# Hybrid decoder trunk: tile 0 of each inner norm turned by VectorE's 32x32 blocks and a trip through DRAM

## The chip, the cores and the metric

The kernel runs on one core of a Trainium2 chip. A core has five engines with a queue each: TensorE (PE; its weight loads are listed as PEld), VectorE (DVE), ScalarE (ACT), GpSimd (POOL) and SyncE (SP), and 16 DMA engines that they share. Each engine works through its instructions in program order and waits on semaphores for the others. The metric is the device time of one execution in microseconds.

## What is computed

A decoder of two layers on x of 512 tokens by 1024 features, all in float32. Each of its four sub-layers stands between two RMS norms:

```
for layer in range(2):
    h = rms_norm(x, norm_mix_pre[layer])
    h = attention(h) if layer == 0 else rglru(h)
    x = x + rms_norm(h, norm_mix_post[layer])
    h = rms_norm(x, norm_ffn_pre[layer])
    h = conv_ffn(h)                       # up 1024 -> 6144, conv, gelu(g) * v, down 3072 -> 1024
    x = x + rms_norm(h, norm_ffn_post[layer])
```

rms_norm divides a token's 1024 features by the root of their mean square and multiplies by a gain per feature. The mixer of layer 0 is a dilated sliding-window attention (24 heads in three groups), that of layer 1 a gated linear recurrence.

## The kernel before

**Layout.** x stays in SBUF as x_sb: four token tiles (t = 0 to 3) of 128 tokens on the partitions, 1024 features along the row. The products of a sub-layer's first step need the features on the partitions, so what a norm gives is kept turned, as hT: eight blocks of 128 features by 512 tokens. Each float32 operand is split into a rounded part and a remainder (hi, lo; hT is such a pair), and each product is three matmuls (mm3, line 253): hi by hi, lo by hi, hi by lo.

**Weights.** They come in chunks of up to 1 MB on SP's queue (load, line 193) into three raw buffers, and are split into hi (ScalarE, line 149) and lo (VectorE, line 150) units by pump (line 167), with at most eight units live.

**Order of the work.** The program is written in the order in which each engine runs it. TensorE's work is cut into steps. After each step tick (line 222) is called: it lets the side jobs that are due go on, and then pump splits more weights if there is room for units. A side job is a generator; the number that it yields is the count of ticks until it goes on.

**The end of a sub-layer.** rows_run (line 422) computes the last product of a sub-layer, token tile by token tile, in PSUM banks called acc. An order written by hand says which tiles take which weight chunks: tiles 0 and 1 finish first, then 2, then 3. When a tile is complete, its norms (line 362) become a side job: postnorm (line 347) adds the normed result to x_sb, and prenorm (line 285) makes the next sub-layer's input. Three of the four sub-layers have a next one: these are the three *inner norms*, after attention, after the first FFN and after the recurrence.

**prenorm and transposed.** rms (line 257) takes the sums of squares on ScalarE and the root's correction on VectorE; the halves of the row, 512 features each, are multiplied by the gain (line 290) and by the root (line 294), into xs[0] and xs[1]. Then the job yields, 4 ticks for tiles 0 to 2 and 3 for tile 3, and transposed (line 298) follows: per half, four TensorE transposes of 128x128 into one PSUM bank (line 302, the tile tr), ScalarE's copy into hT's hi (line 306), and VectorE's subtraction into its lo (line 307).

A step of this stage has 12 matmuls. With the tick at which tile 0's norms are issued called 0, tile 0's transposes are issued at tick 4, tile 1's norms at 3 and its transposes at 7, tile 2's norms at 7, tile 3's at 9. From tick 7 until tile 3's norms are done, no weights are split ("hold", line 363). The next sub-layer's first step (feat_tiles with halves, line 380) follows tick 9: four products on tiles 0 and 1, 24 matmuls of 256 columns each, and then the same four on tiles 2 and 3. Tile 2's transposes stand between the second and the third product of the first round, tile 3's between the third and the fourth.

The gains are loaded on POOL's queue (line 136; on SP's at the end of attention) at the begin of rows_run. POOL also carries small loads of attention: a skewed bias matrix per head (toe, line 586) and, through a DRAM row, a factor per token (crow and cn, lines 813 and 815). The attention's values take a trip through DRAM on SP's queue, to be regrouped (vrows and vp, lines 685 and 698).

SBUF tiles of 128x512 float32 come from one pool of 28 buffers (gen, line 118); PSUM has eight banks.

Of the kernel before, what the change touches and what calls it, by code (L numbers as in the profile page):

```python
# [11 lines left out]
F32 = mybir.dt.float32  # L12
F32R = mybir.dt.float32r
I32 = mybir.dt.int32
AF = mybir.ActivationFunctionType
ALU = mybir.AluOpType
AX = mybir.AxisListType

P = 128
# [55 lines left out]
def kernel(  # L75
# [25 lines left out]
    nc = tc.nc  # L101
# [8 lines left out]
    dp = ctx.enter_context(tc.tile_pool(name="dp", bufs=1, space=bass.MemoryType.DRAM))  # L110
# [3 lines left out]
    def nm(s):  # L114
        uid[0] += 1
        return f"{s}{uid[0]}"

    def gen(dt=F32, s="g"):
        return gp.tile([P, 512], dt, tag="g", name=nm(s))

    def psum(s="ps"):
        return pp.tile([P, 512], F32, tag="ps", name=nm(s))
# [134 lines left out]
    def rms(parts, then):  # L257

        ss, b, v, y, q = small(2), small(2), small(1), small(1), small(1)
        for i, h in enumerate(parts):  # L260
            junk = gen(s="junk")
            nc.scalar.activation(junk, h, AF.Square, accum_out=ss[:, i : i + 1])  # L262
            then(i)
            if not i:
                nc.vector.tensor_scalar(b[:, 0:1], ss[:, 0:1], 1.0 / D, EPS, op0=ALU.mult, op1=ALU.add)
                nc.vector.tensor_scalar(b[:, 1:2], b[:, 0:1], -0.5, None, op0=ALU.mult)
        nc.scalar.activation(y, ss[:, 1:2], AF.Sqrt, scale=1.0 / D, bias=b[:, 0:1])
        nc.vector.scalar_tensor_tensor(v, ss[:, 1:2], -0.5 / D, b[:, 1:2], op0=ALU.mult, op1=ALU.add)
        nc.vector.reciprocal(y, y)
        nc.vector.scalar_tensor_tensor(q, y, v, y, op0=ALU.mult, op1=ALU.mult)  # L270
        nc.vector.scalar_tensor_tensor(y, q, 1.5, y, op0=ALU.add, op1=ALU.mult)
        return y
# [6 lines left out]
    def halves(ap):  # L279
        return [ap[:, 0:512], ap[:, 512:1024]]  # L280

    def new_hT():
        return tuple(htp.tile([P, KD, S], F32R, tag=f"hT{i}", name=nm(f"hT{i}")) for i in range(2))

    def prenorm(t, hT, g, wait):
        xh, gh = halves(x_sb[:, t, :]), halves(g)
        xs = [gen(s="xs") for _ in range(2)]

        def gained(i):
            nc.vector.tensor_tensor(xs[i], xh[i], gh[i], op=ALU.mult)  # L290

        y = rms(xh, gained)
        for i in range(2):
            nc.vector.tensor_scalar(xs[i], xs[i], y, None, op0=ALU.mult)
        yield wait
        transposed(t, xs, hT)

    def transposed(t, xs, hT):
        for i in range(2):
            ps = psum("tr")  # L300
            for k in range(4):
                nc.tensor.transpose(ps[:, k * P : (k + 1) * P], xs[i][:, k * P : (k + 1) * P], ident)  # L302
            ps3 = ps.rearrange("p (k c) -> p k c", k=4)
            hi = hT[0][:, 4 * i : 4 * i + 4, t * P : (t + 1) * P]
            lo = hT[1][:, 4 * i : 4 * i + 4, t * P : (t + 1) * P]
            nc.scalar.activation(hi, ps3, AF.Copy)
            nc.vector.tensor_tensor(lo, ps3, hi.bitcast(F32), op=ALU.subtract)
# [54 lines left out]
    def norms(t, banks, post_g, pre_g, hT):  # L362
        state["hold"] = t >= 2
        postnorm(t, banks, post_g, hT is None)
        if hT is not None:
            yield from prenorm(t, hT, pre_g, 3 if t == 3 else 4)
        if t == 3:
            state["hold"] = False
# [160 lines left out]
    def ffn(layer, hT, post, pre):  # L529
        ca, cc = ffn_cols[layer]  # L530

        def conv(ps, j):
            u = gen(s="u")
            nc.scalar.activation(  # L534
                u, ps, AF.Identity, scale=cc[:, j : j + 1], bias=cc[:, 48 + j : 49 + j]
            )
            for d, wc in ((1, ca[:, 48 + j : 49 + j]), (2, ca[:, j : j + 1])):
                nc.vector.scalar_tensor_tensor(  # L538
                    u[:, d:], ps[:, : S - d], wc, u[:, d:], op0=ALU.mult, op1=ALU.add
                )  # L540
            return u

        gv = []

        def sink(b, ps, j):
            m = b % 2
            if b < 2:
                u = conv(ps, 2 * j + m)
                nc.scalar.activation(u, u, AF.Gelu_apprx_tanh)  # L549
                gv.append(u)  # L550
            else:
                u = conv(ps, 24 + 2 * j + m)
                nc.vector.tensor_tensor(gv[2 * j + m], gv[2 * j + m], u, op=ALU.mult)

        order = [([0, 1, 2, 3], range(9)), ([0], range(9, 12)), ([1], range(9, 12))]
        order += [([2, 3], [9]), ([2], [10, 11]), ([3], [10, 11])]
        prep, run = rows_proj(12, act_split(gv), order, post, pre)
        for j in range(12):
            if j == 11:
                prep(3)  # L560
            feat_tiles(2, hT, lambda b, ps: sink(b, ps, j), j == 0)
        return run()
# [472 lines left out]
    hT = attention(hT, (norm_mix_post, 0), (norm_ffn_pre, 0))  # L1035
    hT = ffn(0, hT, (norm_ffn_post, 0), (norm_mix_pre, 1))
    hT = lru(hT, (norm_mix_post, 1), (norm_ffn_pre, 1))
# [29 lines left out]
```

## Time and profile before

| | us |
|---|---|
| median of three runs | 1474.26 (1474.23 to 1474.28) |
| the profiled execution | 1474.08 |
| its span, first to last instruction | 1472.3 |

| engine | busy share of the span |
|---|---|
| PE | 99% |
| PEld | 84% |
| DVE | 58% |
| ACT | 46% |

The mean TensorE clock granted was 0.999 of full speed. A line of a timeline has the start in us from the span's start, the duration in us, the engine, the line of the kernel, the operation, what it writes and reads, how many of them stand together, and in brackets how long the engine idled before and for whom. A line of a group has count, total busy us and mean ns. A line of a DMA issue has the count, the size of one and the median us from issue to landing. A line of the chain of work that ended last has start, us, engine, tile and line.

### The profile page before, as it was taken

What the parts mean: (1) busy time and instruction counts of PE and PEld (TensorE: products, weight loads), DVE (VectorE), ACT (ScalarE), POOL (GpSimd) and SP (SyncE); (2) the same over time, 40 slices, a digit from 0 to 9 for tenths busy, and PEclk for the clock granted to TensorE, in tenths of its full rate; (3) what the DMA queues carried; (4) which work ended last, traced back from release to release, by engine and by line L of the source; (5) the groups of instructions that cost most, each with busy time, mean ns of one, the idle gap of its engine ahead of it and who ended that gap; (6) DMA issues with size and microseconds to landing.
All of it is one profiled execution on the core that took longest, in us unless ns stands there. A gap on an engine that the chain in (4) does not pass through costs nothing.

```text
span 1472.3 us, 18613 instructions
## 1 busy us (share of the span) xinstructions
PE 1463.5 (99%) x7030; PEld 1231.3 (84%) x7030; DVE 847.1 (58%) x1888; ACT 679.6 (46%) x1538; POOL 43.2 (3%) x111
## 2 busy tenths in 40 slices
PE   9999999999999999999999999999999999999998
PEld 7888888888888898888888888988898888888886
DVE  5645546454545786555555337868785555565333
ACT  7645536262615454433444234489454333444321
POOL 0400001010100000000000000000000000000000
PEclk9999999999999999999999999999999999999999
DMA  6622235343434333223223231341323323223201
GB/s 203 198 65 89 91 91 140 112 137 113 127 125 130 118 115 114 87 91 110 86 106 124 86 99 44 122 138 58 110 97 108 101 86 114 87 87 129 100 0 58
DMA packets 116082, 154.39 MB, mean 105 GB/s; under 512 B 5208, under 2 KB 97592, under 8 KB 115992
## 3 DMA queue, kind: packets, MB, share of 16 engines
q1 hardware_dynamic: 112104, 144.72, 29.9%
q0 software_dynamic: 3296, 7.43, 2.5%
q8 instruction: 55, 0.90, 0.3%
q10 hardware_dynamic: 592, 1.05, 0.2%
q14 instruction: 35, 0.29, 0.1%
HBM read 146.81 MB, written 6.38 MB: 104 GB/s over the span
## 4 chain that ended last, share of the span: by engine, by line
PE 93%; ACT 4%; DVE 3%; issue 1%; DVEq 0%; ACTq 0%
PE ps L255 54%; PE acc L255 24%; PE v L673 7%; PE v L614 1%; DVE xb L879 1%; PE O L821 1%; PE S L774 1%; PE O L759 1%; PE S L724 1%; DVE wlo L150 1%; PE tr L302 1%; ACT sig L900 1%; ACT whi L149 1%; PE PT L808 0%; PE PT L746 0%
## 5 line engine op out<-in xcount | busy, mean ns | idle before, releaser
L255 PE MATMUL ps<-hT,whi 128*128 128x512 f32 (+1 forms) x2752 | 801.6, 375 | 0.0
L255 PEld LDWEIGHTS ps<-hT,whi 128*128 128x128 f32 x2752 | 503.2, 188 | 91.0
L255 PE MATMUL ps<-hT,wlo 128*128 128x512 f32 (+1 forms) x1376 | 515.2, 374 | 0.0
L150 DVE TENSOR_TENSOR wlo<-raw,whi 128x512 fp32r<-128x512 f32 x360 | 230.8, 686 | 190.1 <-ACT whi L149 190.1
L255 PEld LDWEIGHTS ps<-hT,wlo 128*128 128x128 f32 x1376 | 259.1, 188 | 46.5
L149 ACT ACTIVATE whi<-raw 128x512 fp32r<-128x512 f32 x360 | 204.7, 622 | 135.3 <-PE acc L255 120.9
L538 DVE SCALAR_TENSOR_TENSOR u<-ps,cols,u 128x511 f32<-128x511 f32 x192 | 143.8, 749 | 139.9 <-ACT u L534 136.5
L255 PE MATMUL acc<-whi,ahi 128*128 128x512 f32 x512 | 199.9, 390 | 0.0
L255 PE MATMUL acc<-whi,alo 128*128 128x512 f32 x512 | 199.4, 389 | 0.1
L255 PE MATMUL acc<-wlo,ahi 128*128 128x512 f32 x512 | 199.2, 389 | 0.0
L143 ACT ACTIVATE whi<-raw,first_w 128x128 fp32r<-128x128 f32 (+1 forms) x432 | 146.5, 427 | 62.4 <-PE ps L255 53.2
L534 ACT ACTIVATE u<-ps,cols 128x512 f32<-128x512 f32 x96 | 74.8, 779 | 209.3 <-PE ps L255 209.3
L144 DVE SCALAR_TENSOR_TENSOR wlo<-raw,first_w,whi 128x128 fp32r<-128x128 f32 (+1 forms) x432 | 141.9, 391 | 37.5 <-ACT whi L143 37.5
L255 PEld LDWEIGHTS acc<-whi,alo 128*128 128x128 f32 x512 | 96.1, 188 | 20.3 <-DVE alo L150 0.6
L255 PEld LDWEIGHTS acc<-wlo,ahi 128*128 128x128 f32 x512 | 96.2, 188 | 19.9
L255 PEld LDWEIGHTS acc<-whi,ahi 128*128 128x128 f32 x512 | 96.2, 188 | 19.7
L673 PE MATMUL v<-whi,hT 128*128 128x512 f32 x320 | 103.6, 395 | 0.0
L673 PEld LDWEIGHTS v<-whi,hT 128*128 128x128 f32 x320 | 60.1, 188 | 12.1
L549 ACT ACTIVATE u<-u 128x512 f32<-128x512 f32 x48 | 30.3, 632 | 81.2 <-DVE u L538 81.2
L673 PE MATMUL v<-wlo,hT 128*128 128x512 f32 x160 | 62.3, 390 | 0.0
L353 DVE TENSOR_TENSOR post<-acc,gain 128x512 f32<-128x512 f32 x32 | 22.0, 686 | 46.5 <-ACT junk L262 46.5
L601 DVE TENSOR_TENSOR qk<-ps,roots 128x512 f32<-128x512 f32 x24 | 16.6, 690 | 53.4 <-PE ps L255 53.4
(163 smaller groups left out, 969.2 us busy)
## 6 DMA issues: line engine op xcount, KB each, us to landing
raw<-in_ffn_w_up_dram SPq DMA_DIRECT2D x48, 1024.0 KB, 5.2
raw<-in_attn_w_qkv_dram SPq DMA_DIRECT2D x26, 1024.0 KB, 5.0
raw<-in_ffn_w_down_dram SPq DMA_DIRECT2D x24, 1024.0 KB, 5.0
raw<-in_attn_w_qkv_dram SPq DMA_DIRECT2D x19, 512.0 KB, 6.7
raw<-in_lru_w_in_dram SPq DMA_DIRECT2D x8, 1024.0 KB, 5.4
vrows<-v SPq DMA_DIRECT2D x16, 256.0 KB, 3.8
vp<-vrows SPq DMA_DIRECT2D x16, 256.0 KB, 3.7
raw<-in_attn_w_o_dram SPq DMA_DIRECT2D x4, 1024.0 KB, 5.0
```

What stands on the lines that cost most here:

```text
L143: nc.scalar.activation(hi[:, k], raw[:, k], AF.Copy, scale=w)
L144: nc.vector.scalar_tensor_tensor(lo[:, k], raw[:, k], w, hi[:, k].bitcast(F32), op0=ALU.mult, op1=ALU.subtract)
L149: nc.scalar.activation(hi, raw, AF.Copy)
L150: nc.vector.tensor_tensor(lo, raw, hi.bitcast(F32), op=ALU.subtract)
L255: mm(dst, l[a], r[b], start=start and n == 0, stop=stop and n == 2)
L302: nc.tensor.transpose(ps[:, k * P : (k + 1) * P], xs[i][:, k * P : (k + 1) * P], ident)
L353: nc.vector.tensor_tensor(u[i], parts[i], g[:, at[i]], op=ALU.mult)
L534: nc.scalar.activation(u, ps, AF.Identity, scale=cc[:, j : j + 1], bias=cc[:, 48 + j : 49 + j])
L538: nc.vector.scalar_tensor_tensor(u[:, d:], ps[:, : S - d], wc, u[:, d:], op0=ALU.mult, op1=ALU.add)
L549: nc.scalar.activation(u, u, AF.Gelu_apprx_tanh)
L601: nc.vector.tensor_tensor(dst, src, row, op=ALU.mult)
L673: mm(banks[t], hT[a][:, k, t * P : (t + 1) * P], W[b][:, k % 2, :], start=(k, a, b) == (0, 0, 0), stop=(k, a, b) == (KD - 1, 1, 0),)
```

## The change

For tile 0 of an inner norm TensorE's transposes go. Per half of 512 features:

1. `turned`: VectorE transposes each 32x32 block of xs in place of the whole, 128x512 in one instruction, into a tile T whose columns are ordered by (feature block of 32 within 128, block of 128, token within 32). T is written to a new DRAM tensor of 128x512 by one DMA on POOL's queue (256 KB).
2. `fetched`: four DMAs on POOL's queue read it back (64 KB each), each for 32 partitions: 128 rows of 512 bytes. In the tile that they fill, the features are on the partitions, and the columns are ordered by (token block of 32, block of 128 features, token).
3. ScalarE's copy to hi and VectorE's subtraction to lo read this tile in runs of 32 elements, from SBUF.

Steps 1 and 2 are issued right after the scaling (line 294), both writes ahead of the eight reads; step 3 comes six ticks later, where transposed came after four. Per inner norm that is two VectorE transposes and ten DMAs for eight TensorE transposes and two PSUM banks; the copies and subtractions keep their number. Tiles 1 to 3 stay as they were, and so does the first norm at the start of the kernel, which has functions of its own.

```diff
@@ -282,6 +282,26 @@
+    def turned(src, i):
+
+        T = gen(s="T")
+        nc.vector.transpose(
+            T.rearrange("p (c n j) -> p c n j", c=4, j=32), src.rearrange("p (n c j) -> p c n j", c=4, j=32)
+        )
+        d = dp.tile([P, 512], F32, name=nm("turned"))
+        nc.gpsimd.dma_start(d, T)
+        return d
+
+    def fetched(d):
+
+        t = gen(s="ft")
+        for c in range(4):
+            nc.gpsimd.dma_start(
+                t[32 * c : 32 * c + 32].rearrange("j (b x) -> j b x", b=4),
+                d.rearrange("(b j) (c x) -> c j b x", j=32, c=4)[c],
+            )
+        return t.rearrange("p (b n i) -> p n b i", b=4, i=32)
+
     def prenorm(t, hT, g, wait):
@@ -292,8 +312,17 @@
         y = rms(xh, gained)
         for i in range(2):
             nc.vector.tensor_scalar(xs[i], xs[i], y, None, op0=ALU.mult)
-        yield wait
-        transposed(t, xs, hT)
+        if t:
+            yield wait
+            transposed(t, xs, hT)
+            return
+        ds = [turned(h, i) for i, h in enumerate(xs)]
+        xt = [fetched(d) for d in ds]
+        yield 6
+        for i in range(2):
+            hi, lo = (h[:, 4 * i : 4 * i + 4, :P].rearrange("p k (b j) -> p k b j", j=32) for h in hT)
+            nc.scalar.activation(hi, xt[i], AF.Copy)
+            nc.vector.tensor_tensor(lo, xt[i], hi.bitcast(F32), op=ALU.subtract)
```

## The prediction

> **What bounds the kernel now.** I read the page's busy shares first, then TensorE's waits, then the chain of work that ended last around the first inner norm, then the engines' timelines there.
>
> ```profile
> span 1472.3 us, 18613 instructions
> PE 1463.5 (99%) x7030; PEld 1231.3 (84%) x7030; DVE 847.1 (58%) x1888; ACT 679.6 (46%) x1538; POOL 43.2 (3%) x111
> PE warm L995 <- DVE one L1027: 1.5, 1, 1.5
> PE v L614 <- ACT hT L316: 0.2, 1, 0.2
> PE v L614 <- ACT whi L143: 0.2, 1, 0.2
> 482.21 19.06 PE acc L255 x84
> 501.27 0.87 PE tr L302 x8
> 502.14 8.18 PE acc L255 x36
> 897.78 0.87 PE tr L302 x8
> 1055.58 0.87 PE tr L302 x8
> ```
>
> TensorE is busy for 99% of the span; the three lines after that are all of its waits, and all belong to the start. At the norms it never waits. So a TensorE instruction that goes shortens the run by its place in the stream, and another engine matters only if it makes TensorE wait. The chain shows the three groups that the change removes, tile 0's eight transposes in each inner norm, at 0.87 us each. The timeline of TensorE's matmuls around the first group gives the same in another way:
>
> ```profile
> 500.88 0.39 PE L255 MATMUL acc<-whi,alo 128*128 128x512 f32 x1
> 501.11 1.03 PE L302 MATMUL tr<-ident,xs 128*128 128x128 f32 x8
> 501.90 0.48 PE L255 MATMUL acc<-whi,ahi 128*128 128x512 f32 x1
> 502.21 0.40 PE L255 MATMUL acc<-wlo,ahi 128*128 128x512 f32 x1
> 502.45 0.39 PE L255 MATMUL acc<-whi,alo 128*128 128x512 f32 x1
> ```
>
> From 500.88 to 502.45 are 1.57 us. The three ordinary steps in it take 0.227 each (36 in 8.18 us), 0.68 together; 0.89 is left for the group.
>
> **What goes.** 24 transposes in three groups: 3 x 0.87 = 2.61 us off a stream without gaps. It comes back whole if TensorE finds everything else as ready as before, though it arrives 0.87 us earlier at each later step.
>
> **What comes, and when it is needed.** The stage after attention, ScalarE and VectorE:
>
> ```profile
> 504.67 2.19 ACT L149 ACTIVATE whi<-raw 128x512 fp32r<-128x512 f32 x4
> 510.80 1.09 ACT L306 ACTIVATE hT<-tr 128x512 fp32r<-128x512 f32 x2 [3.94 <-PE tr L302]
> 495.95 0.88 DVE L294 TENSOR_SCALAR xs<-xs,s 128x512 f32<-128x512 f32 x2
> 496.75 2.49 DVE L150 TENSOR_TENSOR wlo<-raw,whi 128x512 fp32r<-128x512 f32 x4
> 505.60 1.29 DVE L307 TENSOR_TENSOR hT<-tr,hT 128x512 fp32r<-128x512 f32 x2
> 506.80 2.49 DVE L150 TENSOR_TENSOR wlo<-raw,whi 128x512 fp32r<-128x512 f32 x4
> 511.43 1.29 DVE L307 TENSOR_TENSOR hT<-tr,hT 128x512 fp32r<-128x512 f32 x2 [2.14 <-ACT hT L306]
> 524.72 0.88 DVE L294 TENSOR_SCALAR xs<-xs,s 128x512 f32<-128x512 f32 x2
> 526.00 1.04 PE L302 MATMUL tr<-ident,xs 128*128 128x128 f32 x8
> ```
>
> Tile 0's scaled rows are ready at 496.8 (L294). Its copies into features on partitions now come after six steps of the schedule, not four, so they stand directly ahead of tile 1's (L306 and L307 at 510.80 and 511.43, all 0.87 earlier in the new run: 509.9 and 510.6). ScalarE's two copies take 1.07 there, so the second half must have landed by about **509.3**, 12.5 us after its rows were ready. Behind these copies on ScalarE stand tile 1's copies and tile 2's squares; on VectorE tile 1's subtractions and tile 2's gain product; for these wait the norms of tiles 2 and 3, and for those TensorE.
>
> How late may it be? Tile 3's first scaled half is ready at 525.2 (524.72 and half of 0.88) and TensorE takes it at 526.00: 0.8 us of slack. Lateness up to 0.8 costs nothing; beyond that TensorE stands for the rest; from 1.67 (0.8 + 0.87), landing at 511.0, the stage loses more than it gained.
>
> VectorE: two block transposes, which no row shows. From below the nearest is a one-input operation of this size (L294, 0.44 each), from above the strided add and the scan:
>
> ```profile
> L825 DVE TENSOR_TENSOR o<-O,o 128x512 f32<-128x512 f32 x8 | 8.6, 1069 | 5.5 <-PE O L821 5.4
> L931 DVE TENSOR_TENSOR_SCAN th<-a,th 128x512 f32<-128x512 f32 x8 | 9.8, 1224 | 0.3
> ```
>
> I take 0.6 for each, as for an ordinary operation of this size (L150: 2.49 for four), 1.2 for the two. They push the split of weights and tile 1's norm back by 1.2, which VectorE regains: tile 0's subtractions (1.29) no longer stand at 505.60, and it idled 2.14 before 511.43. By count: tile 1's rows end at 506.8, the four splits at 509.2, tile 0's two subtractions at 510.4, and tile 1's are wanted at 510.6. Nothing is left over, nothing lacks. The copies read SBUF instead of PSUM; L149 (0.55 each) against L306 (0.55 each) says that this is free.
>
> The trip through DRAM is what decides. The issues that resemble it:
>
> ```profile
> vrows<-v SPq DMA_DIRECT2D x16, 256.0 KB, 3.8
> toe<-rowv POOLq DMA_DIRECT2D x16, 64.0 KB, 3.1
> crow<-s POOLq DMA_DIRECT2D x8, 2.0 KB, 1.9
> L586 POOL DMA_DIRECT2D toe<-rowv x24: 535/536/570, 47.9 to 449.1; - x24
> DMA to landing us min/median/max: 3.0/3.2/4.8
> DMA to landing us min/median/max: 2.1/3.8/7.4
> ```
>
> (The last two are the spreads of line L586's transfers and of the vrows and vp transfers.) Per half: one 256 KB write and four 64 KB reads of 512 bytes a row, all on POOL's queue, both writes ahead of the eight reads. The first write is issued 0.6 us after the rows are ready, when the first block transpose ends, and lands 3.8 later, +4.4. Then eight issues of 0.54 one behind the other: the last starts at +8.2 and lands 3.1 later: **+11.3 us, at 508.1, 1.2 before it is needed**. With each piece at its lowest (0.44, 2.1, 3.0) it would be +9.3 (with the 3.8 of the seven issues before); at its highest (1.2, 7.4, 4.8) +17.2, landing at 514.0, 4.7 late: 3.9 us of standing, per stage. I take the middle: 64 KB of 512-byte rows on POOL's queue is exactly what L586 moves, and small POOL writes (crow, 1.9) say that the queue adds little. POOL has nothing else waiting; the next gain loads come at 520.90. SP's queue isn't touched, but shares the engines with this trip: 1 MB of weights follows the first splits (L150 at 496.75), pushed 1.2 back into the reads.
>
> The other two stages, in the same order:
>
> ```profile
> 892.46 0.88 DVE L294 TENSOR_SCALAR xs<-xs,s 128x512 f32<-128x512 f32 x2
> 894.45 0.69 DVE L353 TENSOR_TENSOR post<-acc,gain 128x512 f32<-128x512 f32 x1 [1.11 <-ACT junk L262]
> 907.30 1.09 ACT L306 ACTIVATE hT<-tr 128x512 fp32r<-128x512 f32 x2 [4.63 <-PE tr L302]
> 1050.32 0.88 DVE L294 TENSOR_SCALAR xs<-xs,s 128x512 f32<-128x512 f32 x2
> 1065.10 1.09 ACT L306 ACTIVATE hT<-tr 128x512 fp32r<-128x512 f32 x2 [3.87 <-PE tr L302]
> ```
>
> Rows ready at 893.3 and 1051.2, wanted landed (0.87 and one copy of 0.55 ahead of L306) at 905.9 and 1063.7: 12.5 us each, again 1.2 more than 11.3. VectorE is freer in the middle one (1.11 idle), like attention's in the last.
>
> The sum: -2.61, nothing added. The profiled execution took 1474.08 (span 1472.3 and 1.8 around it) and would take 1471.5; the median of the runs shown is 0.18 higher: **1471.6**, 0.18% less. That lies just within 0.2% (2.95 us, about what a measurement of this kernel tells from no change).
>
> One rule speaks against the change. POOL's issue beside VectorE's scaling, in before:
>
> ```profile
> 920.90 0.53 POOL L136 DMA_DIRECT2D gain<-in_norm_ffn_pre_dram  x1 [2.96 <-DVE s L269]
> 921.23 0.88 DVE L294 TENSOR_SCALAR xs<-xs,s 128x512 f32<-128x512 f32 x2
> gain<-in_norm_ffn_pre_dram POOLq DMA_DIRECT2D x1, 512.0 KB, 3.7
> ```
>
> The issue at 920.90 overlapped L294 and still took 0.53, and its 512 KB landed after 3.7 us: no hold shows. The Trainium skill (SBUF — State Buffer, section SBUF: two separate sides) says that while VectorE runs a two-port fast-mode operation from SBUF to SBUF, GpSimd is locked out of the port they share and can't write a DMA's descriptors. By that rule an issue that meets L294 would wait up to 0.88 us more, which would leave 0.3 of the 1.2 in hand and put the chance of a late trip (below) nearer 0.2; the trace doesn't bear it out here.
>
> **The rivals.**
>
> *The trip comes late (slower).* The copies on ScalarE and VectorE stand in order, so a late landing delays tile 1's copies, then the norms of tiles 2 and 3, and TensorE at 526.00. For: ten transfers on one queue, 1 MB of weights beside them, and single transfers as long as 7.4 and 4.8. Against: the medians leave 1.2 us, then 0.8 of slack. It decides from a landing at +14.2 us. At +17.2 in all three stages: 3 x (3.9 - 0.87) = +9.1, 1483.4; over 0.2% slower needs 2.65 late on average (+15.1).
>
> *VectorE becomes the bound.* With block transposes at 1.22 and subtractions at 1.07 (as L825 for its strides), the count after attention ends at 512.3 where tile 1's subtractions are wanted at 510.6: 1.7 late, 0.9 of standing; the same in the last stage, none in the middle one. -2.61 + 1.8 = -0.8: 1473.5. Against: the pieces read here are runs of 32 elements, not single strided ones.
>
> *TensorE gets back more.* The group's own row lasts 1.03; three times that is 3.1, 1471.2. Against: the rows around the group leave 0.89, since its end lies beside the next product.
>
> **How the numbers follow.** Forecast (1471.3 to 1472.2, within 0.2%) 0.67; VectorE bound (1472.2 to 1473.9, within) 0.11; trip late 0.14, of which 0.12 slower by over 0.2% and 0.02 a partial stall within it; more from TensorE 0.08, faster by over 0.2%. So faster 0.08, within 0.80, slower 0.12. The range goes from 1471.2 (the group's 1.03) to 1474.2 (the VectorE case, and a stage or two of a late trip): what is left out is most of the late trip and the far end of the last case.
>
> **What would show it.** TensorE's count 24 lower, no waits in its list at L302 or at the first products after a norm. If the trip is in time, ScalarE's copies of tile 0 (from the fetched tile) wait for DMA but end before tile 1's transposes start; the last fetch lands within 12.5 us of L294. Wrong would be: tile 1's L306 starting over 0.8 us after TensorE's transposes, TensorE idle at tile 3's transposes, block transposes over 1 us, or POOL issues longer than 0.54.

## The result, and the profile after

The changed kernel takes **1471.51 us** (median, 1471.36 to 1471.59), the kernel before, run beside it, 1474.23: a ratio of 0.9981 with a 95% interval of 0.9974 to 0.9988, 2.7 us less. The profiled execution took 1471.48, its span 1469.7. One execution in this document is left out of its experiment's time: one of four with the copies at tick 8 took 3005.24 us, with TensorE busy for 2995.3 us of it at a recorded clock of 1.0, and why is not known.

The page and TensorE's waits after:

```profile
span 1469.7 us, 18639 instructions
PE 1461.2 (99%) x7006; PEld 1228.7 (84%) x7006; DVE 851.0 (58%) x1894; ACT 682.0 (46%) x1538; POOL 60.1 (4%) x141
PE warm L1024 <- DVE one L1056: 1.5, 1, 1.5
PE v L643 <- ACT hT L345: 0.2, 1, 0.2
PE acc L255 <- DVE alo L150: 0.2, 1, 0.2
```

24 matmuls fewer, and still no wait of TensorE at a norm. VectorE has six instructions more, POOL thirty. The chain of work that ended last, around tile 1's transposes in the three stages (start, us):

```profile
482.23 27.22 PE acc L255 x120
509.44 0.87 PE tr L331 x8
905.04 0.87 PE tr L331 x8
1062.02 0.88 PE tr L331 x8
```

Where two groups interrupted the products there is now one: 27.22 us of products without a break. In before tile 1's groups stood here in the same view:

```profile
510.32 0.87 PE tr L302 x8
906.83 0.87 PE tr L302 x8
1064.63 0.87 PE tr L302 x8
```

In the changed kernel they come 0.88, 1.79 and 2.61 earlier. The gain arrives in three nearly equal parts, each where a group went.

The trip, in the profile after: the stage after attention on ScalarE, then VectorE, then POOL.

```profile
504.93 2.19 ACT L149 ACTIVATE whi<-raw 128x512 fp32r<-128x512 f32 x4
507.71 0.64 ACT L324 ACTIVATE hT<-ft 128x512 fp32r<-128x512 f32 x1 [0.59 <-DMA ft<-turned]
509.78 0.63 ACT L324 ACTIVATE hT<-ft 128x512 fp32r<-128x512 f32 x1 [1.43 <-DMA ft<-turned]
510.31 1.07 ACT L335 ACTIVATE hT<-tr 128x512 fp32r<-128x512 f32 x2
```

```profile
495.97 0.88 DVE L314 TENSOR_SCALAR xs<-xs,s 128x512 f32<-128x512 f32 x2
496.77 1.30 DVE L288 STREAM_TRANSPOSE T<-xs 128x512 f32<-128x512 f32 x2
509.22 0.69 DVE L325 TENSOR_TENSOR hT<-ft,hT 128x512 fp32r<-128x512 f32 x1
510.44 0.69 DVE L325 TENSOR_TENSOR hT<-ft,hT 128x512 fp32r<-128x512 f32 x1 [0.53 <-ACT hT L324]
511.05 1.28 DVE L336 TENSOR_TENSOR hT<-tr,hT 128x512 fp32r<-128x512 f32 x2
524.35 0.88 DVE L314 TENSOR_SCALAR xs<-xs,s 128x512 f32<-128x512 f32 x2
```

```profile
497.77 1.14 POOL L292 DMA_DIRECT2D turned<-T  x2 [31.16 <-DVE T L288]
500.71 4.38 POOL L299 DMA_DIRECT2D ft<-turned  x8 [1.80 <-DMA turned<-T]
```

The second half's copy starts at 509.78; it should have started by 509.38 (510.80 less 0.87, less one copy of 0.55) not to hold tile 1's. So here the trip was 0.4 us late, and tile 1's subtractions (L336, 511.05) come 0.5 later than the 510.56 that 511.43 less 0.87 gives. TensorE doesn't notice: tile 3's first scaled half is ready at 524.8 (524.35 and half of 0.88), and TensorE takes it at 525.10:

```profile
525.10 1.04 PE L331 MATMUL tr<-ident,xs 128*128 128x128 f32 x8
```

Of 0.8 us of slack 0.3 are left. In the other two stages VectorE's subtractions of tile 1 start at 906.14 and 1063.12, as early as TensorE lets them. The 0.4 is what this one profiled execution shows: with the copies two ticks earlier (below), the same reads beside the same weights had all landed by 508.4, and what held the last one here is not shown.

The transfers' landings differ by stage. These are the spreads (least, median, most) of the eight reads, L299, after attention, after the first FFN and after the recurrence:

```profile
DMA to landing us min/median/max: 4.2/5.2/5.8
DMA to landing us min/median/max: 2.1/2.2/2.4
DMA to landing us min/median/max: 3.6/4.9/5.6
```

### The profile page after: what moved, and what is told of

The parts are those of the page before. It is cut to its first block, busy times and chain, and to the rows that moved or that the text cites. A ratio compares the mean times of both kernels' runs of the same rounds, so it can differ in the third digit from the quotient of the medians.

```text
span 1469.7 us, 18639 instructions
## 1 busy us (share of the span) xinstructions
PE 1461.2 (99%) x7006; PEld 1228.7 (84%) x7006; DVE 851.0 (58%) x1894; ACT 682.0 (46%) x1538; POOL 60.1 (4%) x141
## 4 chain that ended last, share of the span: by engine, by line
PE 93%; ACT 4%; DVE 3%; issue 0%; DVEq 0%; ACTq 0%
PE ps L255 55%; PE acc L255 24%; PE v L702 7%; PE v L643 2%; DVE xb L908 1%; PE O L850 1%; PE S L803 1%; PE O L788 1%; PE S L753 1%; DVE wlo L150 1%; ACT sig L929 1%; ACT whi L149 1%; PE tr L331 1%; PE PT L837 0%; PE PT L775 0%
```

## The experiments

The theory: the gain is TensorE's time for three groups of transposes and nothing else; the trip costs nothing as long as the copies of tile 0 don't hold tile 1's by more than 0.8 us; beyond that TensorE stands for the excess. The rivals: the gain comes from what went along with the transposes; or the trip costs something that a larger gain hides; or the margin is of another size. All edits are to the changed kernel, and each time is a median beside runs of the kernel before on the same chip (1474.1 in all).

### The transposes put back

```diff
-        yield 6
+        yield 4
+        for i in range(2):
+            ps = psum("dead")
+            for k in range(4):
+                nc.tensor.transpose(ps[:, k * P : (k + 1) * P], xs[i][:, k * P : (k + 1) * P], ident)
+        yield 2
```

> The changed kernel with TensorE's eight transposes of tile 0 put back at tick 4, into a bank that nobody reads; the trip and its copies stay. Theory (the gain is TensorE's time for three groups, 0.87 us each, and nothing else): back by 2.6 us, 1474.1. Rival (a good part of the gain comes from what went with the transposes: copies that wait for them, banks, the order of the copies): back by clearly less, under 1473.

Measured: **1474.15** (1474.09 to 1474.27), ratio to before 1.000 (0.9991 to 1.0009). The 2.6 us are back, with trip, early copies and late place all kept. The chain of work that ended last shows the group where it stood:

```profile
501.31 0.87 PE dead L325 x8
```

The gain is TensorE's time; in the other two stages the group takes 0.87 as well.

### No trip at all

```diff
-        ds = [turned(h, i) for i, h in enumerate(xs)]
-        xt = [fetched(d) for d in ds]
+        xt = [h.rearrange("p (b n i) -> p n b i", b=4, i=32) for h in xs]
```

> The changed kernel without block transposes and DMAs: tile 0's copies at tick 6 read the scaled rows themselves, so that what they write is not turned (that part of the computation is left out). Theory (the trip lies wholly beside other work): 1471.4 to 1471.5, no different. Rival (the trip, VectorE's block transposes or the late copies cost TensorE something that a larger gain hides): faster by that cost, 1471.2 or less.

Measured: **1471.39** (1471.36 to 1471.56). Six block transposes and 30 DMAs cost at most 0.12 us together. Even that much isn't certain: set against the kernel before on its own chip (1474.12 here, 1474.23 beside the changed kernel), each of the two kernels is 2.7 us faster. A better trip for tile 0 could bring no more than that.

### The copies two ticks earlier

```diff
-        yield 6
+        yield 4
```

> The copies of tile 0 at tick 4, where the transposes stood, not 6. They then stand ahead of the second pair of weight splits on ScalarE and VectorE. Theory (a late landing holds what is queued behind it, 0.8 us of it free): after attention tile 1's subtractions come 3.0 late, after the recurrence 1.3, after the first FFN 0.2, so TensorE stands 2.2 + 0.5 + 0 and the time is about 1474.2. Rival (the place of the copies in the queues doesn't matter as long as the data are there before the next products): 1471.5.

Measured: **1473.14** (1472.55 to 1473.65): slower than the changed kernel by 1.6 us, not by 2.7. The place in the queues matters; I had the lateness too large. VectorE and TensorE after attention:

```profile
508.38 1.41 DVE L325 TENSOR_TENSOR hT<-ft,hT 128x512 fp32r<-128x512 f32 x2 [1.45 <-ACT hT L324]
509.71 2.49 DVE L150 TENSOR_TENSOR wlo<-raw,whi 128x512 fp32r<-128x512 f32 x4
512.12 1.28 DVE L336 TENSOR_TENSOR hT<-tr,hT 128x512 fp32r<-128x512 f32 x2
525.95 1.09 PE L331 MATMUL tr<-ident,xs 128*128 128x128 f32 x8 [0.65 <-DVE xs L314]
```

The second half's copy followed the first without a break (1.35 us for the two, from 507.71), so tile 1's subtractions were 1.6 late (512.12 against 510.56), not 3.0. Less the 0.8 of slack that is 0.8, and TensorE's transposes of tile 3 start 0.85 later than 525.10. In the last stage TensorE waited 0.58 at the same place. With four ticks, as the transposes had, about 60% of the gain is lost: the two more ticks are part of the change.

### A second hop through DRAM

```diff
+    def hop(d):
+        e = dp.tile([P, 512], F32, name=nm("hop"))
+        nc.gpsimd.dma_start(e, d)
+        return e
...
+        ds = [hop(d) for d in ds]
         xt = [fetched(d) for d in ds]
```

> A copy from DRAM to DRAM (256 KB per half) between write and reads, which lengthens the trip by about 3 us. Theory: the second half lands about 3.3 us after the 12.5 that it has after attention, 1.7 after the recurrence, 0.7 after the first FFN; TensorE stands for what is over 0.8, 2.5 + 0.9 + 0, about 1474.9. Rival (the margin is much larger than counted): 1471.5. Rival (no slack of 0.8): 3.3 + 1.7 + 0.7 less 0.4 that is late already, 1476.8.

Measured: **1488.43** (1484.90 to 1489.44), a miss by 13 us. The hop and the reads behind it, after attention:

```profile
hop<-turned POOLq DMA_DIRECT2D x2, 256.0 KB, 5.0
DMA to landing us min/median/max: 2.1/2.4/6.1
516.01 0.63 ACT L330 ACTIVATE hT<-ft 128x512 fp32r<-128x512 f32 x1 [5.62 <-DMA ft<-hop]
531.12 1.09 PE L337 MATMUL tr<-ident,xs 128*128 128x128 f32 x8 [2.42 <-DVE xs L319]
```

The hop took 5.0 us where I had put 3, and pushed the second half's last reads to where the next 1 MB of weights runs: up to 6.1 us (the second line, the spread of the eight reads), so the copy starts at 516.0. That is 6.6 after 509.38; less 0.8 is 5.8, and tile 3's transposes start 6.0 after 525.10. So the rule of lateness less 0.8 holds at this size as well, and what was wrong is the length of the trip. It is not the hop alone: after the first FFN the hop took 2.9, about what I had put, and still the last read took 5.6 beside the next weights. The three stages lose 6.0, 3.6 and 3.9 us by the starts of tile 3's transposes, which makes this profiled execution (1485.02) 13.5 us longer than the changed kernel's. The median lies 3.4 above it; the three longer executions, from 1488.43 to 1489.44, have a mean clock of 0.994 to 0.998, this one 0.999; no profile shows where those three lost their time.

### More block transposes

```diff
         xt = [fetched(d) for d in ds]
+        for h in (xs[0], xs[1], xs[0], xs[1]):
+            T = gen(s="idle")
+            nc.vector.transpose(
+                T.rearrange("p (c n j) -> p c n j", c=4, j=32), h.rearrange("p (n c j) -> p c n j", c=4, j=32)
+            )
```

> Four more block transposes on VectorE per inner norm, right behind the two, into tiles that nobody reads: 4 x 0.62 = 2.5 us more of VectorE, the trip itself not delayed. Theory (VectorE has regained the first 1.2 and has little left after attention and after the recurrence): tile 1's subtractions come 2.4 late in both, TensorE stands 1.6 each, none after the first FFN: about 1474.6. Rival (VectorE still has room there): 1471.5.

Measured: **1474.65** (1474.56 to 1475.15), as expected. VectorE, then TensorE after attention and after the recurrence:

```profile
512.72 1.28 DVE L341 TENSOR_TENSOR hT<-tr,hT 128x512 fp32r<-128x512 f32 x2
```

```profile
526.55 1.09 PE L336 MATMUL tr<-ident,xs 128*128 128x128 f32 x8 [1.37 <-DVE xs L314]
1080.70 1.09 PE L336 MATMUL tr<-ident,xs 128*128 128x128 f32 x8 [1.42 <-DVE xs L314]
```

Tile 1's subtractions are 2.2 late, TensorE stands 1.4; there is no such wait after the first FFN, where VectorE had room. VectorE is the second bound of this stage: it could take the first two block transposes because tile 0's subtractions left their old place, and little beyond (2.4 us more made tile 1's subtractions 2.2 late).

### The copies two ticks later

```diff
-        yield 6
+        yield 8
```

> The copies of tile 0 at tick 8: behind tile 1's copies and tile 2's norms. Theory (the trip is long over, but the copies then come only when ScalarE and VectorE are through with tile 2, about 3 us after the first product wants them): TensorE stands some 3.1 us in each of the three stages, about 1480.8. Rival (any place ahead of the products does, and later is safer): 1471.5.

Measured: **1486.90** (1486.80 to 1487.97), or 1487.4 as the median with the fourth execution, slower still than the 1480.8 that the standing gives. To see where the rest went the same kernel ran once more:

> The kernel with the copies of tile 0 at tick 8 once more, for its timeline: it took 1487.4, 6.6 us more than 3.1 us of standing per stage would give. Theory (once TensorE has stood for about 3 us its granted clock falls, as in the kernel with tile 1 on the trip, where it was 0.67 to 0.73 in the 5 us after the wait): three waits of 3 to 4 us at the first products of the next sub-layer, each followed by some 5 us at a clock of about 0.7, 1.5 us more each. Rival (the copies come still later than counted): waits of 5 us or more and a clock of 1.00.

Measured: **1484.04** (1483.83 to 1484.24). TensorE after attention (the waits at the first product and at the next), then stretches after attention and after the recurrence (start and end, length, then busy time and count of PE, PEld, DVE, ACT and POOL, the clock granted to TensorE, DMA share, GB/s):

```profile
516.99 0.38 PE L255 MATMUL ps<-hT,whi 128*128 128x256 f32 x1 [1.21 <-ACT hT L324]
518.95 0.39 PE L255 MATMUL ps<-hT,whi 128*128 128x256 f32 x1 [1.58 <-DVE hT L325]
```

```profile
515.00:520.00 5.00, 2.21 (x14) 1.56 (x13) 4.86 (x14) 3.57 (x11) 0.00 (x0) 1.00 0.00 0
520.00:525.00 5.00, 5.00 (x45) 5.00 (x44) 4.76 (x18) 1.98 (x6) 0.83 (x2) 1.00 0.31 105
1075.00:1080.00 5.00, 2.35 (x10) 2.15 (x11) 4.83 (x17) 2.95 (x10) 0.00 (x0) 0.70 0.02 3
1080.00:1085.00 5.00, 5.00 (x30) 5.00 (x30) 4.75 (x17) 1.69 (x5) 0.56 (x1) 0.62 0.31 105
1077.00:1083.70 6.70, 5.67 (x26) 5.67 (x27) 6.49 (x20) 2.67 (x10) 0.56 (x1) 0.50 0.24 79
```

The last product of attention starts at 515.39, so without a wait the second one here would start at 515.74 (0.227 later for the first, 0.12 for the next, which has half the columns). It starts at 518.95: 3.2 us of standing, near the 3.1 expected, and the same in the other two stages (waits of 1.2 and 1.57 us there too). That gives 1481.1; most of the remaining 2.9 is the clock. After the recurrence the two stretches of 5 us have a mean clock of 0.70 and 0.62, and in the second 30 matmuls ran instead of 45. The last row shows what lies behind these means: half the clock, 0.50, for 6.7 us, and full clock before and behind. From the first product to tile 3's transposes this stage takes 13.96 us, where the same piece takes 11.42 after attention: 2.5 us. After attention, with the same wait, the clock stayed at 1.00. My expectation of a lower clock after all three was wrong for this run: it fell once. In the first runs of this kernel the mean clock was 0.994, here 0.997, which fits their longer time; they left no profile to show it.

### Weights only after the trip

```diff
+        last = dp.tile([P, 1], F32, name=nm("last"))
+        nc.sync.dma_start(last, t[:, 0:1])
         return t.rearrange("p (b n i) -> p n b i", b=4, i=32)
```

> A small DMA on SP's queue that reads a column of each fetched tile stands ahead of the next weights, so that these start only when the trip is over. Theory (the reads landed after 5.2 us after attention and 4.9 after the recurrence because 1 MB of weights ran beside them, and after 2.2 after the first FFN, where none did): the reads land after 2.2 to 2.6 in all stages, the trip ends about 2 to 3 us earlier, and the time stays at 1471.5 since the trip was hidden anyway. Rival (the reads are slow by themselves in these stages): 4.5 or more again.

Measured: 1476.68 (1474.18 to 1482.15), inconclusive: in the first two stages seven of the eight reads landed within 2.3 us, but the last took 7, because of the probe itself, as it seems: the DMA of 128 single elements took 6.9 to 9.4 us. So it was made shorter:

```diff
+        last = dp.tile([4, P], F32, name=nm("last"))
+        nc.sync.dma_start(last, t[0:P:32, 0:P])
```

> As the experiment with the small DMA on SP's queue ahead of the next weights, but that DMA now reads four rows of 512 bytes of the fetched tile (one from each read) where it read 128 single elements and took 7 to 9 us itself. Theory (1 MB of weights beside the reads makes them slow, and the trip is hidden either way): all reads land after 2.1 to 2.9 us, the second half is there by 507.5 after attention, no copy waits for it, and the time is 1471.4 to 1471.6. Rival (the second half's reads are late by themselves, or weights that start 3 us later cost as much as the trip gains): a copy that waits past 509, or a time over 1472.

Measured: **1471.57** (1471.41 to 1471.62). The eight reads after attention, and ScalarE's copies:

```profile
DMA to landing us min/median/max: 2.1/2.1/2.3
507.01 1.13 ACT L326 ACTIVATE hT<-ft 128x512 fp32r<-128x512 f32 x2
```

Without weights beside them the reads take 2.1 us, not 5.2; the copies wait for nothing and stand back to back at 507.01, 2.3 us earlier at their end, and tile 1's subtractions, which start at 510.55, aren't late any more. The time is the same, for the trip was hidden before. The slowness of the reads comes from the weights beside them, and it doesn't matter here.

### Tile 1 as well

```diff
-        if t:
+        if t > 1:
...
-            hi, lo = (h[:, 4 * i : 4 * i + 4, :P].rearrange("p k (b j) -> p k b j", j=32) for h in hT)
+            hi, lo = (h[:, 4 * i : 4 * i + 4, t * P : (t + 1) * P].rearrange("p k (b j) -> p k b j", j=32) for h in hT)
```

> Tile 1 takes the same trip, its copies six ticks after its norms (tick 9). It takes 0.87 us more off TensorE per stage, but tile 1's rows are ready only some 9 us before the first product wants them, and the trip takes 9 to 13. Theory: the copies land 3 to 5 us late and TensorE stands for that, net +2 to +4 per stage, about 1480 (1477 to 1484). Rival (the trip hides for tile 1 too): 1471.5 - 2.6 = 1468.9.

Measured: **1483.89** (1483.12 to 1484.78), at the upper end. TensorE's waits, the copy after attention for which its first product waited, and a stretch behind the wait in each of the three stages:

```profile
PE ps L255 <- ACT hT L324: 7.7, 3, 3.1
PE ps L255 <- DVE hT L325: 1.3, 3, 0.5
518.64 0.63 ACT L324 ACTIVATE hT<-ft 128x512 fp32r<-128x512 f32 x1 [0.99 <-DMA ft<-turned]
520.00:523.30 3.30, 3.11 (x14) 3.11 (x15) 2.93 (x11) 1.78 (x6) 0.48 (x1) 0.50 0.00 0
919.30:922.70 3.40, 3.40 (x18) 3.40 (x17) 3.26 (x11) 1.27 (x4) 0.56 (x1) 0.50 0.10 14
1079.80:1083.10 3.30, 2.86 (x14) 2.83 (x14) 2.34 (x6) 2.08 (x6) 0.00 (x0) 0.50 0.02 5
```

The kernel is 12.4 us slower than the changed one although it has 2.6 us of transposes less: 15.0 to be accounted for, of which the waits are 9.0. The clock fell to half in all three stages, for 3.3 to 3.4 us each. That costs some 1.7 us a stage, about 5 together (an estimate: half of these stretches); about 1 is left open.

The trip hides for tile 0 because its rows are ready some 19 us before the next sub-layer; tile 1's are ready only 9 us before. But the long trip is not the whole of the wait. At tick 9 tile 1's copies also stand behind tile 2's norms, as tile 0's do with eight ticks, where TensorE stood 3.2 with the trip long over. After attention ScalarE came free at 517.65 and waited 0.99 for the first fetched half, of 3.0 that TensorE waited for that copy. No run here has tile 1's copies at an earlier tick, so the two causes aren't separated.

## Why the prediction was right

Point by point, by its own steps.

*What goes: 3 x 0.87 = 2.61.* Measured 0.88, 0.91 and 0.82 at tile 1's groups in the three stages: 2.61 together, 2.60 between the two profiled executions (1474.08 and 1471.48), 2.7 between the medians. The transposes put back bring back 2.6. Right, and shown.

*Block transposes at 0.6, bounds 0.44 and 1.22.* They take 0.69 alone and a pair 1.30. Near the value taken. The rival built on the upper bound was added up wrong by a little: 1.24 more for the transposes and 0.85 for the subtractions on top of 510.4 end at 512.5, not 512.3, which gives 1473.9 in place of 1473.5. It didn't come: tile 0's subtractions took 0.69, not 1.07.

*VectorE regains the 1.2: "Nothing is left over, nothing lacks".* Right: tile 1's rows end at 506.9 (predicted 506.8), and when 2.5 us more were added, TensorE stood 1.4 in the two tight stages and not in the free one.

*The trip at +11.3, bounds +9.3 and +17.2.* This sum was too short: after attention the copy started at +12.9, past the +12.5 that was allowed, so the 1.2 us in hand were gone. Two of its pieces were wrong, in opposite directions. The writes landed after 2.4, not 3.8: they lie near the least (2.1) of the vrows and vp transfers taken for them, not near the median. The reads took 5.2 after attention and 4.9 after the recurrence, not 3.1, and 2.2 after the first FFN. The prediction named the weights that would be pushed into the reads, but put no price on them; the run without them shows the price, 3 us.

*The 0.8 us of slack.* This carried the result after attention, where the trip was 0.4 late. Lateness less 0.8 met TensorE's delay in three experiments: 1.6 late gave 0.85, 2.2 gave 1.4, 6.6 gave 6.0. That the time held is therefore luck in part: the margin that the prediction added up for the trip was used up, and the slack behind it, which it had read rightly, took the rest with 0.3 us left.

*The signs of being wrong.* After attention three of them came, though the time held. Tile 1's copy started 0.87 us after its transposes in the chain (510.31 after 509.44; in before 0.48); the last read landed later than 12.5 us after the rows; and POOL's issues took 0.55. The one that bears on the time, TensorE idle at tile 3's transposes, didn't come.

*The price of the late rival.* A late trip costs what was said (one stage of the second hop: 3.9 us foreseen for a landing 4.7 late, 6.0 measured for 6.6). But a wait at the next sub-layer's first products can cost more than its length, since the clock may fall after it (to 0.50 for 3.3 to 6.7 us in two of the experiments); the prediction had no such term.

*The rule on the shared port.* POOL's issues of the trip took 0.55 us at the median, as in before (0.54), with VectorE busy for 1.9 to 2.0 of each 2 us beside them after attention; the writes landed after 2.3 to 2.6. But none of these issues after attention met the scaling. After the first FFN one did, the seventh read's:

```profile
L299 POOL DMA_DIRECT2D ft<-turned x1: 704/704/704, 899.6 to 899.6; - x1
899.72 0.88 DVE L314 TENSOR_SCALAR xs<-xs,s 128x512 f32<-128x512 f32 x2
```

Overlapped by the scaling nearly from end to end, it took 0.70, and the issues of the same kind took 0.71 to 0.78 in seven of the experiments. The read landed after 2.2 all the same, and it isn't the last, so the time didn't change. The Trainium skill (SBUF — State Buffer, section SBUF: two separate sides) says that GpSimd is locked out of the port that it shares with VectorE during VectorE's two-port fast-mode operations and can't write a DMA's descriptors. The trace agrees with it in direction, with 0.15 to 0.23 us more and not the up to 0.88 that the prediction worked out.

*TensorE gets back more* (1.03 a group): not so, the three groups gave 0.82 to 0.91.

## What to carry to other kernels

Where one engine is busy throughout, an instruction taken off it is worth its step in the stream, and what replaces it costs nothing as long as the engines that take it over find their queues as early as before: count the time between when the data are ready and when the instruction behind the waiting one is wanted, not when the result itself is wanted. That sets the place in the program too: four ticks lost about 60% of the gain and eight ticks lost it several times over, with the same trip. And stop where the margin ends: what hid for tile 0 cost 12 us when tile 1 took the trip too.

## What was not expected of the hardware

Reads of 64 KB on POOL's queue landed after 2.1 us alone and after 5.2 (both medians) beside 1 MB of weights on SP's queue. A DMA of 128 single elements from SBUF to DRAM took 7 to 9 us, and with it in flight one of the reads beside it took 7.

TensorE's granted clock fell to half after waits at the first products: to 0.50 for 3.3 to 3.4 us in all three stages with tile 1 on the trip, and for 6.7 us after one of three waits of about 3 us with eight ticks. Values such as 0.62 and 0.70 in stretches of 5 us are means over half and full clock. What decides whether it falls isn't settled by these runs. The length of the wait alone isn't it: after the first FFN with tile 1 on the trip the waits of 1.51 and 0.34 us, with one product between, were followed by a fall, while waits of 1.2 and 1.57 with eight ticks were followed by none in two stages of three. In the second hop's profiled execution, where no single wait was longer than 2.4 us, the mean clock stayed at 0.999.
